# One-core transformer block in split fp32: the lists' matmuls a step deeper, their key products on ScalarE, gate tiles of a pair loaded ahead, the last two query tiles interleaved, the static split and the overflow set-up moved

## The chip, the core and the metric

The kernel runs on one core of a Trainium2 chip. Engines are named as in the profile: PE (TensorE), DVE (VectorE), ACT (ScalarE), POOL (GpSimd), SP (SyncE, which here only issues DMAs). The metric is the device time of one launch in microseconds (us); the median of the runs counts.

## The reference, cut to what matters

A block of attention and a PEER layer (product-key mixture of single-row experts), then a second block (gated convolution and linear recurrence). All of it is fp32 on 256 tokens of width 2048. The change touches the PEER layer:

```python
q = (xt @ w_query).reshape(T, 8, 2, 128)
scores = jnp.einsum('thpc,hpnc->thpn', q, sub_keys)      # 128 keys per half
vals, idx = lax.top_k(scores, 16)                        # per token, head, half
cand = vals[..., 0, :, None] + vals[..., 1, None, :]     # 256 candidates
top_vals, top_c = lax.top_k(cand, 16)
experts = i1 * 128 + i2                                  # 128 (expert, gate) pairs per token
gates = softmax(top_vals)
hdn = gelu(einsum('ted,td->te', expert_down[experts], x))
y = einsum('te,ted->td', gates * hdn, expert_up[experts])
```

## The kernel before

A product in fp32 is made of three: every operand is split into a high part (a cast to fp32r) and a low part (the rest), and PE multiplies high by high, high by low and low by high. `Stream` (line 63) feeds the weights: a unit is 128 x 2048 fp32 (1 MB), loaded by SP into one of three buffers `raw`, and then split in two halves into `whl` (five buffers): the high part is an ACT cast (line 74), the low part a DVE subtraction (line 75). So a half is ready at most five halves ahead of its use. `fm` (line 88, matmuls on lines 100 to 102) multiplies one unit with all 256 tokens in 48 matmuls; `tm` (line 106) does it with tokens as rows.

The PEER layer (`phase_peer`) takes no gather for its first product: it computes the hidden value of all 16384 experts for all 256 tokens. Its parts, in the order of PE:

1. 16 query tiles (loop on line 898), each `fm`, then the scores of the tile before. The top-k work (DVE and POOL) is cut in steps in a queue `k.bg`; `pump_by` (line 187) takes as many steps after each unit as a credit in us, and the `us` that each step names, allow. In the last tile (g 15) the activations `k.act` are replaced, quarter by quarter, by their scaled form (`split`, lines 213 and 214), since the next units need that form.
2. 128 down units in groups of four (loop on line 1013; a group `j` is 512 experts). `hidden` (line 978) writes the gelu of a unit into `ghs` (three buffers, one per group). In the background run, first, the steps `place_steps` (matmuls, line 710) that scatter each token's gates into a full table `g_d` in HBM. As long as it isn't complete, finished groups go to `gh_d` in HBM and into the queue `late` (23 groups). Once it is (`state["placed"]`), `catch_up` (line 996) brings the late ones back, one or two at a time: POOL loads the gates of a pair of groups (`gt<-g_d`, line 875, 1 MB, for every second group) and the group (`ght<-gh_d`, line 890), multiplies (`times`, line 880) and stores to `hm_d` (line 883). The last nine groups, called direct here (23 to 29, then 31 and 30), are multiplied from `ghs`; the gates of their pair are loaded by `hidden` right before the first of the pair is multiplied, into one buffer `gtd`. All of that stands in POOL's one queue in program order. Group JS = 31 isn't stored: its product is split into `hst` (lines 213 and 214), the left operand of the first four up units.
3. From down unit 103 on, the background builds lists of the experts in use: 32 steps `lists_steps` (line 848). Step q issues `lists_hot(q+2)` (two DVE comparisons, tiles `oe` and `oa`, lines 826 and 828), `lists_keys(q+1)` (tile `ob`: one half an ACT product, line 836, the other a DVE product, line 837) and `lists_fill(q)` (four PE matmuls, line 845). What is left after unit 123 is drained.
4. A branch over code that isn't run with these inputs (`overflow`, lines 1058 to 1090): each engine loads a register (line 1063) and jumps (line 1064). DVE prepares two tiles for it first, `ld` (line 1060) and `xe` (line 1062).
5. 104 up units (matmuls on line 1117): four static ones (they use `hst`), then 100 whose rows POOL gathers by the lists (line 1047).

Of the kernel before, what the change touches and what calls it, by code (L numbers as in the profile page):

```python
# [26 lines left out]
NE = 128  # L27
# [4 lines left out]
JS = 31  # L32
# [15 lines left out]
class Stream:  # L48
# [29 lines left out]
    def next(self):  # L78

        self.i += 1  # L80
        while self.done < min(2 * self.i + HL - 2, 2 * len(self.units)):
            self._half()
        return self.w.pop(self.i - 1)

    def used(self):
# [477 lines left out]
def phase_peer(k, A):  # L563
# [5 lines left out]
    with ExitStack() as ctx:  # L569
# [250 lines left out]

        def lists_hot(q):
            cs = slice(4 * q, 4 * q + 4)
            a = pw.tile([128, 4, 128], F32R, name="oa", tag="oa", bufs=3)
            e = pw.tile([128, 4, KT], F32, name="oe", tag="oe")
            rp = L["rp"]
            nc.vector.tensor_tensor(e, iota[:, None, :KT].to_broadcast([128, 4, KT]),
                                    rp[:, 0, cs, None].to_broadcast([128, 4, KT]), op=OP.is_equal)
            nc.vector.tensor_tensor(a, iota[:, None, :].to_broadcast([128, 4, 128]),
                                    rp[:, 1, cs, None].to_broadcast([128, 4, 128]), op=OP.is_equal)
            hot[q] = [a, e]  # L830

        def lists_keys(q):
            cs = slice(4 * q, 4 * q + 4)
            b = pw.tile([128, 4, 2, KT], F32R, name="ob", tag="ob")
            e = hot[q][1]
            nc.scalar.mul(b[:, :, 0, :], e, pi)
            nc.vector.tensor_mul(b[:, :, 1, :], e, iota[:, cs, None].to_broadcast([128, 4, KT]))
            hot[q][1] = b

        def lists_fill(q):  # L840
            if q == 0:
                L["ps"] = bank(k, "bg")
            a, b = hot.pop(q)
            for j in range(4):
                nc.tensor.matmul(L["ps"][:, :2 * KT], a[:, j, :], b[:, j].rearrange("p e r -> p (e r)"),
                                 start=q + j == 0, stop=q == 31 and j == 3)

        def lists_steps(q):
            if q + 2 < 32:
                lists_hot(q + 2)  # L850
            if q + 1 < 32:
                lists_keys(q + 1)
            lists_fill(q)

        def indices(v, n, nm):

# [38 lines left out]
            nc.vector.tensor_sub(lo[:, t], x[:, t], hi[:, t].bitcast(F32))  # L895

        scaled = []
        for g in range(16):
            w = st.next()
            acc = bank(k, "acc")[:, :256]  # L900
            if g == 15:
                for q in range(4):
                    fm(k, acc, w, k.act, part=(4 * q, 4 * q + 4))
                    qs = slice(4 * q, 4 * q + 4)
                    split(k, k.act[0][:, qs, :], k.act[1][:, qs, :], scaled.pop(0))
            elif g == 0:
# [12 lines left out]
            if g == 4:  # L919
                row_bc(k, Rb, r)  # L920
            qT = pw.tile([128, 256], F32, name="qT", tag="qT")
            nc.scalar.copy(qT, acc)
            if g < 2:
                pump(k)
            else:
                pump_by(k, 3.2)
            if 6 <= g <= 12 and g % 2 == 0:

                q = g // 2 - 3
                x = pw.tile([128, 4, 256], F32, name="xr", tag="ob" if q == 3 else "ghs", bufs=2 if q == 3 else 3)  # L930
                a, b = [o[:, 4 * q:4 * q + 4, :].bitcast(F32) for o in k.act]
                nc.gpsimd.tensor_add(x, a, b)
                nc.gpsimd.tensor_mul(x, x, Rb[:, None, :].to_broadcast([128, 4, 256]))
                scaled.append(x)
            k.bg.appendleft(step(0.0, lambda g=g, qT=qT: scores(g, qT)))
            if g % 2:
                k.bg.extend(topk_steps(g // 2))
        state = {}

        def prepare():  # L940

            def lag():
# [28 lines left out]
            yield step(1.5, lambda: lists_hot(0))  # L971
            yield step(2.2, lambda: (lists_hot(1), lists_keys(0)))
            for q in range(32):
                yield step(2.2, lambda q=q: lists_steps(q))
            yield lag()
            yield step(1.5, lists_end)
        k.bg.extend(prepare())
# [3 lines left out]
        def hidden(j, a, gh, acc):  # L981
# [7 lines left out]
            if state.get("g") != j // 2:  # L989
                state["g"], state["gt"] = j // 2, load_g(j // 2, "gtd")  # L990
            times(gh, state["gt"], j)
            if j == JS:
                hst = state["hst"] = pp.tile([128, 2, 4, 256], F32R, name="hst", tag="gst%d" % (JS // 2 % 2))
                split(k, hst[:, 0], hst[:, 1], gh)
            else:
                store(j, gh)

# [57 lines left out]
        k.gather = gather  # L1055


        def overflow():
            d = L["d"]
            nc.vector.tensor_scalar(d, d, -128.0 * KT, None, op0=OP.add)  # L1060
            ex = pw.tile([128, 128], F32, name="xe", tag="xe", bufs=1)
            nc.vector.tensor_scalar(ex, iota, 128.0, pi, op0=OP.mult, op1=OP.add)
            turns = nc.values_load(L["nx"][0:1, 1:2], min_val=0, max_val=NE)
            with k.tc.If(turns > 0), k.tc.For_i(0, turns, 1) as _:
                ps = bank(k, "bg")
                for c in range(NE):
                    a = pw.tile([128, 128], F32, name="xa", tag="xa")
                    nc.vector.tensor_scalar(a, iota, d[:, c:c + 1], None, op0=OP.is_equal)
                    nc.tensor.matmul(ps[:, :1], a, ex[:, c:c + 1], start=c == 0, stop=c == NE - 1)
                v = pp.tile([128, 1], F32, name="xv")  # L1070
                nc.vector.tensor_copy(v, ps[:, :1])
                idx = indices(v, 1, "x")
                x = pw.tile([128, 2048], F32, name="xu", tag="xu", bufs=1)
                get(x, up, idx[:, 0, :], NE * 128)
                y = pw.tile([128, 256], F32, name="xh", tag="hr", bufs=4)
                get(y, hm_d, idx[:, 1, :], JS * 512 + 1)
                h = pw.tile([128, 2, 256], F32R, name="xs", tag="hh", bufs=3)
                split(k, h[:, 0], h[:, 1], y)
                for c in range(4):
                    cs = slice(c * 512, (c + 1) * 512)  # L1080
                    w = pw.tile([128, 2, 512], F32R, name="xw", tag="xw", bufs=1)
                    split(k, w[:, 0], w[:, 1], x[:, cs])
                    for t in range(2):
                        ts = slice(t * 128, (t + 1) * 128)
                        o = bank(k, "bg")
                        for i, (p, q) in enumerate(((0, 0), (0, 1), (1, 0))):
                            nc.tensor.matmul(o, h[:, p, ts], w[:, q], start=i == 0, stop=i == 2)
                        nc.vector.tensor_add(k.h[:, t, cs], k.h[:, t, cs], o)
                nc.vector.tensor_scalar(d, d, -128.0, None, op0=OP.add)
        overflow()  # L1090

        accs = [[bank(k, "bg" if c < 2 else "acc") for t in range(2)] for c in range(4)]
# [619 lines left out]
```

## Time and profile before

| | us |
|---|---|
| median of three runs | 2737.36 |
| lowest run | 2737.03 |
| the profiled execution: its time | 2741.86 |
| its span, from the first to the last instruction | 2740.1 |
| PE busy in that span | 2634.3 (96%) |
| DVE busy | 1829.5 (67%) |
| ACT busy | 1411.4 (52%) |
| POOL busy | 738.6 (27%) |

Times in the rows are us from the start of the span. Where PE waits, two things cost: the wait itself and, after a longer one, matmuls at the lower granted clock. An engine's share over the whole span says little here, since the stages have different limits: the query tiles lie at about 464 to 579 us, the down units at 573 to 1408, the lists at 1186 to 1362, and the up units begin at 1421.5.

### The profile page before, as it was taken

What the parts mean: (1) busy time and instruction counts of PE and PEld (TensorE: products, weight loads), DVE (VectorE), ACT (ScalarE), POOL (GpSimd) and SP (SyncE); (2) the same over time, 40 slices, a digit from 0 to 9 for tenths busy, and PEclk for the clock granted to TensorE, in tenths of its full rate; (3) what the DMA queues carried; (4) which work ended last, traced back from release to release, by engine and by line L of the source; (5) the groups of instructions that cost most, each with busy time, mean ns of one, the idle gap of its engine ahead of it and who ended that gap; (6) DMA issues with size and microseconds to landing.
All of it is one profiled execution on the core that took longest, in us unless ns stands there. A gap on an engine that the chain in (4) does not pass through costs nothing. (4 is left out here: it accounts for less than half of the span.)

```text
span 2740.1 us, 44958 instructions
## 1 busy us (share of the span) xinstructions
PE 2634.3 (96%) x18008; PEld 2409.1 (88%) x18008; DVE 1829.5 (67%) x2685; ACT 1411.4 (52%) x2302; POOL 738.6 (27%) x779
## 2 busy tenths in 40 slices
PE   8999999989999999989759999999999999999997
PEld 8977778989999999989748888887999999999886
DVE  5554455899777877688826666666568775555555
ACT  6344455544566666434325555556665544444453
POOL 0001011532000000255625555645145540000000
PEclk9999999999999999999879999999999999999999
DMA  7433435456688888989847888885544445555553
GB/s 290 169 123 139 155 118 188 155 171 214 208 279 274 279 279 289 312 308 340 303 146 271 297 292 293 293 300 173 191 167 156 153 154 204 185 185 188 185 192 127
DMA packets 95268, 599.11 MB, mean 219 GB/s; under 512 B 11536, under 2 KB 11664, under 8 KB 31952
## 3 DMA queue, kind: packets, MB, share of 16 engines
q1 hardware_dynamic: 53696, 381.05, 39.6%
q0 software_dynamic: 36608, 200.23, 21.6%
q10 hardware_dynamic: 4752, 14.92, 1.5%
q8 instruction: 143, 2.34, 0.3%
q14 instruction: 69, 0.57, 0.1%
HBM read 532.19 MB, written 47.19 MB: 211 GB/s over the span
## 5 line engine op out<-in xcount | busy, mean ns | idle before, releaser
L75 DVE TENSOR_TENSOR whl<-raw,whl 128x1024 fp32r<-128x1024 f32 (+2 forms) x917 | 1188.5, 1306 | 633.7 <-ACT whl L74 623.0
L74 ACT CAST whl<-raw 128x1024 fp32r<-128x1024 f32 (+2 forms) x917 | 954.3, 1048 | 734.2 <-PE acc L102 381.4
L100 PE MATMUL acc<-act,whl 128*128 128x256 f32 x3840 | 1083.4, 282 | 17.8 <-ACT whl L74 17.6
L101 PE MATMUL acc<-act,whl 128*128 128x256 f32 x3840 | 1081.8, 282 | 9.1 <-DVE act L214 8.7
L102 PE MATMUL acc<-act,whl 128*128 128x256 f32 x3840 | 1081.6, 282 | 0.8 <-DVE whl L75 0.8
L100 PEld LDWEIGHTS acc<-act,whl 128*128 128x128 f32 x3840 | 729.4, 190 | 20.2 <-ACT whl L74 17.8
L101 PEld LDWEIGHTS acc<-act,whl 128*128 128x128 f32 x3840 | 730.1, 190 | 10.0 <-DVE act L214 8.9
L102 PEld LDWEIGHTS acc<-act,whl 128*128 128x128 f32 x3840 | 733.3, 191 | 1.3 <-DVE whl L75 1.3
L1117 PE MATMUL acc<-whl,hh 128*128 128x512 f32 x864 | 218.2, 396 | 0.0
L1117 PE MATMUL bg<-whl,hh 128*128 128x512 f32 x864 | 217.9, 396 | 0.0
L118 PE MATMUL acc<-whl,act 128*128 128x512 f32 (+1 forms) x512 | 198.2, 387 | 6.9 <-ACT whl L74 6.9
L119 PE MATMUL acc<-whl,act 128*128 128x512 f32 (+1 forms) x512 | 196.1, 383 | 4.0 <-DVE whl L75 3.9
L1117 PEld LDWEIGHTS bg<-whl,hh 128*128 128x128 f32 x864 | 162.5, 188 | 39.3
L1117 PEld LDWEIGHTS acc<-whl,hh 128*128 128x128 f32 x864 | 162.4, 188 | 39.2
L120 PE MATMUL acc<-whl,act 128*128 128x512 f32 (+1 forms) x512 | 195.8, 382 | 0.8 <-DVE act L217 0.8
L1047 POOL DMA_INDIRECT raw<-in_up,idx_l x100 | 134.1, 1341 | 150.5 <-DVE hh L895 77.6
L118 PEld LDWEIGHTS acc<-whl,act 128*128 128x128 f32 x512 | 97.5, 190 | 28.7 <-ACT whl L74 7.4
L119 PEld LDWEIGHTS acc<-whl,act 128*128 128x128 f32 x512 | 97.5, 190 | 24.4 <-DVE whl L75 5.8
L738 POOL DMA_DIRECT2D g_d<-gst x16 | 8.9, 556 | 395.7 <-DVE gst L722 395.7
L120 PEld LDWEIGHTS acc<-whl,act 128*128 128x128 f32 x512 | 97.4, 190 | 20.2 <-DVE act L217 1.0
L1047 POOL DMA_INDIRECT hr<-hm_d,idx_l x100 | 104.4, 1044 | 31.0 <-issue 30.7
L700 ACT ACTIVATE ob<-oe,sl_g 128x128 fp32r<-128x128 f32 x256 | 81.5, 391 | 8.1 <-ACT ghs L982 6.5
(407 smaller groups left out, 3071.5 us busy)
## 6 DMA issues: line engine op xcount, KB each, us to landing
raw<-in_down SPq DMA_DIRECT2D x128, 1024.0 KB, 6.3
raw<-in_w_cv SPq DMA_DIRECT2D x32, 1024.0 KB, 4.8
raw<-in_w_gg SPq DMA_DIRECT2D x32, 1024.0 KB, 4.8
raw<-in_w_dil SPq DMA_DIRECT2D x24, 1024.0 KB, 4.9
gt<-g_d POOLq DMA_DIRECT2D x17, 1024.0 KB, 10.7
raw<-in_w_out SPq DMA_DIRECT2D x16, 1024.0 KB, 4.8
raw<-in_w_pq SPq DMA_DIRECT2D x16, 1024.0 KB, 4.9
g_d<-gst POOLq DMA_DIRECT2D x16, 1024.0 KB, 7.8
```

The source lines that it names most:

```text
L74: nc.scalar.copy(hi[:, s], r[:, s])
L75: nc.vector.tensor_sub(lo[:, s], r[:, s], hi[:, s].bitcast(F32))
L100: k.nc.tensor.matmul(acc, hi[:, f], x, start=j == 0, stop=False)
L101: k.nc.tensor.matmul(acc, hi[:, f], y, start=False, stop=False)
L102: k.nc.tensor.matmul(acc, lo[:, f], x, start=False, stop=j == nk - 1)
L118: k.nc.tensor.matmul(accs[t], ah[:, kk, ts], hi[:, m], start=st, stop=False)
L119: k.nc.tensor.matmul(accs[t], ah[:, kk, ts], lo[:, m], start=False, stop=False)
L120: k.nc.tensor.matmul(accs[t], al[:, kk, ts], hi[:, m], start=False, stop=sp)
L700: nc.scalar.mul(b[:, j, 0, :], e[:, j, :], slot["g"][:, 0, 4 * q + j:4 * q + j + 1].bitcast(F32))
L738: nc.gpsimd.dma_start(g_d[g], x.rearrange("p i t -> p (i t)"))
L1047: nc.gpsimd.indirect_dma_start(out=out, out_offset=None, in_=table, in_offset=bass.IndirectOffsetOnAxis(ap=idx, axis=0), bounds_check=n - ...
L1117: nc.tensor.matmul(accs[2 * s + c][t], x[:, ts], y[:, c * 512:(c + 1) * 512], start=i == 0 and x is hh and y is hi, stop=last_ and i == N - 1)
```

## The change

Six edits. (a) `lists_steps(q)` issues the matmuls of step q-1, so each product is made two steps ahead of its use; a fourth buffer for `oa` and a third for `ob` come from tiles that are free by then. (b) The DVE product of the keys goes to ACT: six ACT operations per step (two of 128 x 2 x 100, four of 128 x 100) in place of one of 128 x 400; a step's cost for the credit falls from 2.2 to 1.7. (c) After a direct group, if the next group belongs to another pair, the gates of that pair are loaded at once. (d) Query tiles 14 and 15 run interleaved by quarters, and each quarter of `k.act` is split as soon as both have used it; behind tiles 14 and 15 one background step is taken instead of 3.2 us of them. (e) The split into `hst` is issued three units later. (f) `ld` and `xe` are made inside the branch.

```diff
+    def peek(self):
+        self.i += 1
         return self.w.pop(self.i - 1)
...
         def lists_hot(q):
-            a = pw.tile([128, 4, 128], F32R, name="oa", tag="oa", bufs=3)
+            a = (pp.tile([128, 4, 128], F32R, name="oa", tag="sl_g") if q % 4 == 3 else
+                 pw.tile([128, 4, 128], F32R, name="oa", tag="oa", bufs=3))
...
         def lists_keys(q):
-            b = pw.tile([128, 4, 2, KT], F32R, name="ob", tag="ob")
+            if q % 3 == 2:
+                b = [pw.tile([128, 2, 2, KT], F32R, name="ob", tag="oh") for _ in range(2)]
+            else:
+                b = pw.tile([128, 4, 2, KT], F32R, name="ob", tag="ob")
+                b = [b[:, 0:2], b[:, 2:4]]
             e = hot[q][1]
-            nc.scalar.mul(b[:, :, 0, :], e, pi)
-            nc.vector.tensor_mul(b[:, :, 1, :], e, iota[:, cs, None].to_broadcast([128, 4, KT]))
+            for i in range(2):
+                nc.scalar.mul(b[i][:, :, 0, :], e[:, 2 * i:2 * i + 2], pi)
+            for j in range(4):
+                nc.scalar.mul(b[j // 2][:, j % 2, 1, :], e[:, j, :], float(4 * q + j))
...
         def lists_steps(q):
...
-            lists_fill(q)
+            if q >= 1:
+                lists_fill(q - 1)
...
         for g in range(16):
...
+            if g == 14:
+                pair = [(acc, w), (bank(k, "acc")[:, :256], st.peek())]
                 for q in range(4):
-                    fm(k, acc, w, k.act, part=(4 * q, 4 * q + 4))
+                    for o, x in pair:
+                        fm(k, o, x, k.act, part=(4 * q, 4 * q + 4))
+                    if q == 1:
+                        st.used()
+                        st.used()
                     qs = slice(4 * q, 4 * q + 4)
                     split(k, k.act[0][:, qs, :], k.act[1][:, qs, :], scaled.pop(0))
...
+            elif g < 14:
+                pump_by(k, 3.2)
             else:
-                pump_by(k, 3.2)
+                pump(k)
...
             times(gh, state["gt"], j)
+            n = ORDER.index(j) + 1
+            if n < 32 and ORDER[n] // 2 != j // 2:
+                state["g"], state["gt"] = ORDER[n] // 2, load_g(ORDER[n] // 2, "gtd")
             if j == JS:
                 hst = state["hst"] = pp.tile([128, 2, 4, 256], F32R, name="hst", tag="gst%d" % (JS // 2 % 2))
-                split(k, hst[:, 0], hst[:, 1], gh)
+                after(k, 3, lambda: split(k, hst[:, 0], hst[:, 1], gh))
...
         def overflow():
             d = L["d"]
-            nc.vector.tensor_scalar(d, d, -128.0 * KT, None, op0=OP.add)
-            ex = pw.tile([128, 128], F32, name="xe", tag="xe", bufs=1)
-            nc.vector.tensor_scalar(ex, iota, 128.0, pi, op0=OP.mult, op1=OP.add)
             turns = nc.values_load(L["nx"][0:1, 1:2], min_val=0, max_val=NE)
-            with k.tc.If(turns > 0), k.tc.For_i(0, turns, 1) as _:
+            with k.tc.If(turns > 0):
+                nc.vector.tensor_scalar(d, d, -128.0 * KT, None, op0=OP.add)
+                ex = pw.tile([128, 128], F32, name="xe", tag="xe", bufs=1)
+                nc.vector.tensor_scalar(ex, iota, 128.0, pi, op0=OP.mult, op1=OP.add)
+                with k.tc.For_i(0, turns, 1) as _:
+                    overflow_tile(d, ex)
```

The body of the loop is the new function `overflow_tile`, otherwise unchanged. Lines after the change are 5 to 33 higher (line 880 is 893, line 213 is 218).

Three places in the order of the instructions. First DVE, from the first weight subtractions beside query tile 14 on (`act` are the activations, `xr` their scaled form, `vals`, `tk`, `idx` and `oh` belong to the top-k steps). Before:

```order
L75 TENSOR_TENSOR whl<-raw,whl 128x1024 x2
L597 MAX vals<-sc 128x8
L598 MATCH_REPLACE tk<-vals,sc 128x128
L599 MAX_INDEX idx<-vals,sc 128x8
L632 TENSOR_TENSOR oh<-abf,cst 128x512
L602 MAX vals<-tk 128x8
L603 MAX_INDEX idx<-vals,tk 128x8
L75 TENSOR_TENSOR whl<-raw,whl 128x1024
L214 TENSOR_TENSOR act_82<-xr,act_81 128x1024 x3
L75 TENSOR_TENSOR whl<-raw,whl 128x1024
L214 TENSOR_TENSOR act_82<-xr,act_81 128x1024
```

And at the same place on DVE in the changed kernel:

```order
L75 TENSOR_TENSOR whl<-raw,whl 128x1024
L219 TENSOR_TENSOR act_82<-xr,act_81 128x1024
L75 TENSOR_TENSOR whl<-raw,whl 128x1024 x2
L219 TENSOR_TENSOR act_82<-xr,act_81 128x1024 x2
L75 TENSOR_TENSOR whl<-raw,whl 128x1024
L219 TENSOR_TENSOR act_82<-xr,act_81 128x1024
L75 TENSOR_TENSOR whl<-raw,whl 128x1024 x4
```

The four splits moved ahead of the top-k step, between the weight subtractions; everything ahead of this piece stands as before.

Second POOL, at the end of the down units, from the last late groups (`ght`) to the last direct ones (`ghs`: 28 and 29, then 31 and 30). Before:

```order
L880 TENSOR_TENSOR ght<-ght,gt 128x1024
L883 DMA hm_d<-ght 128x4x256
L875 DMA gt<-g_d 128x16x128
L880 TENSOR_TENSOR ghs<-ghs,gt 128x1024
L883 DMA hm_d<-ghs 128x4x256
L880 TENSOR_TENSOR ghs<-ghs,gt 128x1024
L883 DMA hm_d<-ghs 128x4x256
L875 DMA gt<-g_d 128x16x128
L880 TENSOR_TENSOR ghs<-ghs,gt 128x1024 x2
L883 DMA hm_d<-ghs 128x4x256
L1063 TENSOR_LOAD nx
```

The same end of POOL's queue in the changed kernel (group 28 stands further up, three late groups earlier):

```order
L893 TENSOR_TENSOR ght<-ght,gt 128x1024
L896 DMA hm_d<-ght 128x4x256
L893 TENSOR_TENSOR ght<-ght,gt 128x1024
L896 DMA hm_d<-ght 128x4x256
L893 TENSOR_TENSOR ghs<-ghs,gt 128x1024
L888 DMA gt<-g_d 128x16x128
L896 DMA hm_d<-ghs 128x4x256
L893 TENSOR_TENSOR ghs<-ghs,gt 128x1024 x2
L896 DMA hm_d<-ghs 128x4x256
L1115 TENSOR_LOAD nx
```

The gate load of the last pair moved past one instruction, the store of group 29; the product of group 31 still follows it directly.

Third ACT, from the gelu of down unit 123 to the branch (`hst` is the static split, `nx` the branch's count). Before:

```order
L982 ACTIVATE ghs<-acc 128x256
L213 CAST hst<-ghs 128x1024
L74 CAST whl<-raw 128x1024 x2
L982 ACTIVATE ghs<-acc 128x256
L74 CAST whl<-raw 128x1024 x2
L982 ACTIVATE ghs<-acc 128x256
L74 CAST whl<-raw 128x1024 x2
L982 ACTIVATE ghs<-acc 128x256 x2
L1063 TENSOR_LOAD nx
```

And in the changed kernel, from the same gelu on:

```order
L1007 ACTIVATE ghs<-acc 128x256
L74 CAST whl<-raw 128x1024 x2
L1007 ACTIVATE ghs<-acc 128x256
L74 CAST whl<-raw 128x1024 x2
L1007 ACTIVATE ghs<-acc 128x256
L218 CAST hst<-ghs 128x1024
L74 CAST whl<-raw 128x1024 x2
L1007 ACTIVATE ghs<-acc 128x256 x2
L1115 TENSOR_LOAD nx
```

The static cast moved behind four weight casts and two gelus; two weight casts still stand behind it. Elsewhere on PE, the last of the `place_steps` matmuls stand behind 93 down units (before: 91), and the first list matmuls behind 106 (before: 103).

## Rows read from the trace of the kernel before

**Rows 1.** PE's waits: us in total, times, longest.

```profile
PE bg L845 <- DVE ob L837: 26.2, 9, 6.7
PE acc L100 <- ACT whl L74: 17.6, 1, 17.6
PE bg L1117 <- DVEq L1064: 13.3, 1, 13.3
PE acc L101 <- DVE act L214: 8.7, 1, 8.7
PE bg L845 <- ACT ob L836: 5.3, 1, 5.3
```

**Rows 2.** Stretches: length, busy us (instructions) by engine, PE clock, DMA share, GB/s.

```profile
1130.00:1140.00 10.00, 10.00 (x88) 10.00 (x87) 2.40 (x2) 3.96 (x6) 2.28 (x3) 1.00 1.00 314
1250.00:1260.00 10.00, 8.44 (x73) 8.30 (x72) 9.90 (x12) 3.42 (x5) 5.72 (x3) 1.00 1.01 410
1130.00:1396.00 266.00, 219.25 (x1762) 217.39 (x1760) 195.15 (x193) 92.50 (x129) 139.69 (x101) 0.92 0.87 307
1186.00:1362.00 176.00, 144.51 (x1134) 143.00 (x1134) 151.78 (x138) 66.49 (x95) 103.99 (x75) 0.92 0.92 327
```

**Rows 3.** Groups of POOL's products, 1120 to 1400 us: busy, mean ns | idle before.

```profile
L880 POOL TENSOR_TENSOR ght<-ght,gt 128x1024 f32<-128x1024 f32 x23 | 63.6, 2764 | 51.9 <-DMA ght<-gh_d 51.7
L880 POOL TENSOR_TENSOR ghs<-ghs,gt 128x1024 f32<-128x1024 f32 x8 | 20.0, 2499 | 62.5 <-DMA gt<-g_d 31.5 <-issue 18.5 <-ACT ghs L982 12.5
```

**Rows 4.** Timeline of POOL: start, duration, engine, operation, [idle before].

```profile
1130.83 1.21 POOL L875 DMA_DIRECT2D gt<-g_d  x1 [7.03 <-DMA g_d<-gst]
...
1146.66 2.52 POOL L880 TENSOR_TENSOR ght<-ght,gt 128x1024 f32<-128x1024 f32 x1 [13.55 <-DMA ght<-gh_d]
...
1307.20 1.17 POOL L875 DMA_DIRECT2D gt<-g_d  x1
...
1317.76 2.63 POOL L880 TENSOR_TENSOR ght<-ght,gt 128x1024 f32<-128x1024 f32 x1 [4.79 <-DMA ght<-gh_d]
...
1321.48 1.16 POOL L875 DMA_DIRECT2D gt<-g_d  x1
...
1379.36 2.37 POOL L880 TENSOR_TENSOR ghs<-ghs,gt 128x1024 f32<-128x1024 f32 x1 [9.43 <-DMA gt<-g_d]
...
1386.47 1.17 POOL L875 DMA_DIRECT2D gt<-g_d  x1
1393.95 2.33 POOL L880 TENSOR_TENSOR ghs<-ghs,gt 128x1024 f32<-128x1024 f32 x1 [6.31 <-DMA gt<-g_d]
```

**Rows 5.** Tile gt: its DMAs from issue to landing.

```profile
DMA to landing us min/median/max: 7.3/10.7/19.5
```

**Rows 6.** Timeline of DVE: the last sum over the placed gates.

```profile
1138.83 2.29 DVE L744 TENSOR_REDUCE F<-fsum 128x128 f32<-128x2048 f32 x1 [6.28 <-DMA fsum<-gst]
```

**Rows 7.** Timeline of ACT, DVE and PE: from the static split to the up units.

```profile
1396.32 1.04 ACT L213 CAST hst<-ghs 128x1024 fp32r<-128x1024 f32 x1 [28.20 <-POOL ghs L880]
...
1398.54 2.36 DVE L75 TENSOR_TENSOR whl<-raw,whl 128x1024 fp32r<-128x1024 f32 x2
...
1415.12 0.52 DVE L1062 TENSOR_SCALAR xe<-cst 128x128 f32<-128x128 f32 x1 [7.77 <-DMA hm_d<-ghs]
...
1421.53 0.77 PE L1117 MATMUL bg<-whl,hst 128*128 128x512 f32 x1 [13.26 <-DVEq L1064]
```

**Rows 8.** Timeline of DVE and PE around the last query tile.

```profile
563.53 2.36 DVE L75 TENSOR_TENSOR whl<-raw,whl 128x1024 fp32r<-128x1024 f32 x2
...
569.69 3.48 DVE L214 TENSOR_TENSOR act<-xr,act 128x1024 fp32r<-128x1024 f32 x3
...
579.10 0.27 PE L590 MATMUL bg<-keys,qT 128*128 128x128 f32 x1
```

**Rows 9.** Groups of ACT's key products (the first from 1186 to 1362 us).

```profile
L836 ACT ACTIVATE ob<-oe,cst 128x400 fp32r<-128x400 f32 x31 | 19.2, 622 | 27.2 <-DVE oe L826 21.1 <-PE bg L845 6.1
...
L700 ACT ACTIVATE ob<-oe,sl_g 128x128 fp32r<-128x128 f32 x256 | 81.5, 391 | 8.1 <-ACT ghs L982 6.5
```

More of the change, by code (lines that the diff above doesn't have):

```diff
@@ L82, in next @@
             self._half()
+        return self.w.pop(self.i - 1)
+    def peek(self):
+        self.i += 1
         return self.w.pop(self.i - 1)
@@ L844, in lists_fill @@
             for j in range(4):
-                nc.tensor.matmul(L["ps"][:, :2 * KT], a[:, j, :], b[:, j].rearrange("p e r -> p (e r)"),
+                nc.tensor.matmul(L["ps"][:, :2 * KT], a[:, j, :], b[j // 2][:, j % 2].rearrange("p e r -> p (e r)"),
                                  start=q + j == 0, stop=q == 31 and j == 3)
@@ L897, in phase_peer @@
         scaled = []
+        pair = []
         for g in range(16):
-            w = st.next()
-            acc = bank(k, "acc")[:, :256]
-            if g == 15:
-                for q in range(4):
-                    fm(k, acc, w, k.act, part=(4 * q, 4 * q + 4))
+            if g < 15:
+                w = st.next()
+                acc = bank(k, "acc")[:, :256]
+            if g == 14:
+                pair = [(acc, w), (bank(k, "acc")[:, :256], st.peek())]
+                for q in range(4):
+                    for o, x in pair:
[3 more added lines that the diff above has]
+                        st.used()
                     qs = slice(4 * q, 4 * q + 4)
                     split(k, k.act[0][:, qs, :], k.act[1][:, qs, :], scaled.pop(0))
+            elif g == 15:
+                acc = pair[1][0]
             elif g == 0:
@@ L970, in prepare @@
             yield step(1.6, lists_split)
[L971 to L974, printed above, removed]
+            yield step(1.7, lambda: lists_hot(0))
+            yield step(1.7, lambda: (lists_hot(1), lists_keys(0)))
+            for q in range(33):
+                yield step(1.7, lambda q=q: lists_steps(q))
             yield lag()
@@ L1055, in phase_peer, with overflow_tile @@
         k.gather = gather
+        def overflow_tile(d, ex):
+            ps = bank(k, "bg")
+            for c in range(NE):
+                a = pw.tile([128, 128], F32, name="xa", tag="xa")
+                nc.vector.tensor_scalar(a, iota, d[:, c:c + 1], None, op0=OP.is_equal)
+                nc.tensor.matmul(ps[:, :1], a, ex[:, c:c + 1], start=c == 0, stop=c == NE - 1)
+            v = pp.tile([128, 1], F32, name="xv")
+            nc.vector.tensor_copy(v, ps[:, :1])
+            idx = indices(v, 1, "x")
+            x = pw.tile([128, 2048], F32, name="xu", tag="xu", bufs=1)
+            get(x, up, idx[:, 0, :], NE * 128)
+            y = pw.tile([128, 256], F32, name="xh", tag="hr", bufs=4)
+            get(y, hm_d, idx[:, 1, :], JS * 512 + 1)
+            h = pw.tile([128, 2, 256], F32R, name="xs", tag="hh", bufs=3)
+            split(k, h[:, 0], h[:, 1], y)
+            for c in range(4):
+                cs = slice(c * 512, (c + 1) * 512)
+                w = pw.tile([128, 2, 512], F32R, name="xw", tag="xw", bufs=1)
+                split(k, w[:, 0], w[:, 1], x[:, cs])
+                for t in range(2):
+                    ts = slice(t * 128, (t + 1) * 128)
+                    o = bank(k, "bg")
+                    for i, (p, q) in enumerate(((0, 0), (0, 1), (1, 0))):
+                        nc.tensor.matmul(o, h[:, p, ts], w[:, q], start=i == 0, stop=i == 2)
+                    nc.vector.tensor_add(k.h[:, t, cs], k.h[:, t, cs], o)
+            nc.vector.tensor_scalar(d, d, -128.0, None, op0=OP.add)
@@ L1058, in overflow @@
         def overflow():
             d = L["d"]
-            nc.vector.tensor_scalar(d, d, -128.0 * KT, None, op0=OP.add)
-            ex = pw.tile([128, 128], F32, name="xe", tag="xe", bufs=1)
-            nc.vector.tensor_scalar(ex, iota, 128.0, pi, op0=OP.mult, op1=OP.add)
             turns = nc.values_load(L["nx"][0:1, 1:2], min_val=0, max_val=NE)
-            with k.tc.If(turns > 0), k.tc.For_i(0, turns, 1) as _:
[L1065 to L1089, printed above, removed]
```

1 line of the change is left out of this document (removed).

## Prediction

> **What bounds the kernel now.** I read PE's waits first, since PE is busy for 96% of the span. Seventy us of it can be named [rows 1]: list matmuls wait for DVE's key product (26.2 us, nine times) and for ACT's (5.3), one weight unit waits 17.6 us for ACT's cast, the up units wait 13.3 us for DVE's branch, and the last query tile waits 8.7 us for a split. The second view is the table of stretches [rows 2]: over the lists PE's granted clock is 0.92, a mean between the two levels (2.4 and 1.2 GHz), where quiet stretches show 1.00. That is 8% of 176 us, 14.1 us of matmuls at the lower level after waits. So PE could win 70 + 14 us at most, if nothing else came late.
>
> The third view shows what else comes late. ACT's static split idles 28.20 us for POOL [rows 7], and behind it in ACT's order stand two weight casts: that is PE's 17.6. POOL multiplies the last late groups while PE is nearly through the down units [rows 4]: POOL is tens of us behind PE, in one queue, and its idle time is DMA waits: 51.9 us for late groups and 62.5 for gates of direct groups [rows 3]. One cycle of two late groups lasts from 1307.20 to 1321.48, 14.3 us, of which 4.79 are a visible wait and the rest two products, two stores and three issues [rows 4]. So POOL's chain sets when group 31's product is there, 1396.28 (1393.95 + 2.33), and from that the up units follow. Below, T is the end of this product in the changed kernel.
>
> **The change, part by part.** *Lists (a, b).* Each key product is made one step earlier, so the 26.2 and the 5.3 go; with them most of the 14.1 us of slow clock. DVE loses 32 products. ACT gains, per step, at least the removed form (0.62 us, the mean of one 128 x 400 product) and at most 2 x 0.622 + 4 x 0.391 = 2.8 us, by the nearest rows [rows 9]. The instructions issued back to back there cost 0.32 each (81.5/256), which gives about 2 us. That is 32 x 2 = 64 us more on ACT, which is busy 66.49 of the 176 us [rows 2]; weights are cast up to five halves ahead, so I cost it at nothing. Without that cover it would be a wait of 2 us a step. On PE these edits bring the end of the down units forward: it lies at 1408.27 (1421.53 - 13.26 [rows 7]), and less 26.2, 5.3, 14.1 and the 17.6 of the next part it becomes about 1345.
>
> *Static split moved (e).* It no longer stands ahead of four of the six weight casts, and the two behind it are for weights that the down units don't need. The 17.6 go as a wait for weights. But the up units need `hst`, thus T: the stall isn't gone if T is late, it moves from the last down unit to the first up unit.
>
> *Gates ahead (c).* What is T? The last placing matmuls stand two units later, 48 matmuls each: 5.45 us a unit at 88 in 10 us, 6.0 at 1762 in 219 with slow clock [rows 2]; with 5.6 that is 11.2 us. DVE's last sum ends at 1141.12 (1138.83 + 2.29 [rows 6]); plus 11.2, plus a gate landing of 10.7 [rows 5], plus a product of 2.4: the first direct product ends at 1165.4. In the old trace the work from the first gate load (1130.83) to the last pair's load (1368.76 = 1379.36 - 9.43 - 1.17) takes 237.9 us [rows 4]. From this go the direct waits before the last two, 62.5 - 9.43 - 6.31 = 46.7, since their gates are now loaded a pair ahead; the first wait, 15.83 (1146.66 - 1130.83), since the late groups are loaded beside the first direct one; and to it come three waits for late groups that the long direct waits had covered, 3 x 4.79 = 14.4. That leaves 189.8 and ends at 1355.2. The last pair gains nothing: its gates are asked for right behind 29's product and needed at once, so 2.4 + 10.7 + 2.35 follow, T = 1371.
>
> The other bound is the traffic. From 1130 to 1396 the core moved 307 GB/s, 81.7 MB [rows 2]; with the last store of `g_d` and `fsum` (1 MB each) it is 83.8 MB, and the share was 0.87. At full share and the same work, 307/0.87 = 353 GB/s, it takes 237 us, T = 1367; at the 327 GB/s of the list stretch, 256 us, T = 1386 [rows 2]. I take T = 1378, between the two and near the chain's sum, as prefetches ask for more at once and landings should not get shorter. The ends kept are 1355 and 1396.
>
> The Trainium skill ("DMA: Bandwidth & Descriptors", section Specifications) gives a limit of about 358 GB/s of HBM traffic for a core; by it the bytes above would need 234 us, an estimate that gives T = 1364. The 353 GB/s at full share agree, and one stretch with 410 GB/s [rows 2] stands above it, so the rule is no floor here.
>
> POOL's late products take 2764 ns on average and 2.33 us where nothing runs beside them [rows 3, 4]; if the absence of DVE's key products made them all short, 23 x 0.43 = 10 us at most would come off the chain, T = 1361. The Trainium skill ("SBUF — State Buffer", section Who interferes with whom) says that DVE and GpSimd share one port pair and that this is an exclusive lock; by it the 32 products that leave DVE speak for that shorter chain, but the weight subtractions, far more numerous, stay.
>
> *From T to the up units.* Before, product to the end of DVE's second weight subtraction is 1398.54 + 2.36 - 1396.28 = 4.6 us [rows 7]: the cast, two weight casts and the subtractions, the same instructions in both. *The branch (f)*: without `xe` DVE no longer waits 7.77 us for the store; what remains is 1421.53 - 1415.64 = 5.9 us from the end of `xe` (1415.12 + 0.52) to the first up matmul [rows 7]. So the up units start at T + 10.5 = 1388.5 where before it was 1421.53. The gain is **33 us**, and PE waits some 43 us, from 1345 to 1388.
>
> *Query tiles (d).* DVE's order from 563.53 on now alternates weight subtractions (2.36/2 = 1.18) and splits (3.48/3 = 1.16) [rows 8]: four of each, 9.4 us, then a last group of 12 matmuls (1.4 us by 88 in 10 us [rows 2]) end at 574.4, where before the scores of the last tile come at 579.10 [rows 8]. I take **4 us**. The ends are 0 (the top-k steps moved behind make another wait) and 8.7 plus as much slow clock again at a quarter, about 11.
>
> Sum: 2740.1 - 33 - 4 = 2703.1 of span. The profiled execution, 2741.86, is 4.5 above the median 2737.36, so against the median: 2737.36 - 37 = **2700**.
>
> **Rivals.**
> *A: POOL's chain keeps up and PE loses all its waits.* 26.2 + 5.3 + 17.6 + 8.7, of the 13.3 all but the branch's 5.9, and the 14.1 of clock: 79.3 us, 2658. For it: 115 us of POOL's DMA waits [rows 3] and one stretch of 410 GB/s. Against it: it needs T at 1340, thus 83.8 MB in 210 us, 399 GB/s throughout, while another stretch at full share moved only 314 [rows 2]. Chance 0.15.
> *B: the loads are the bound and nothing comes earlier.* The DMA engines show a share of 0.92 to 1.0 in the list stretch [rows 2]; a load asked for earlier then lands no earlier, the placing is two units late, and T stays about 1396. Gain: 1421.53 - (1396 + 10.5) = 15, plus 4: 2718. Against it: the 46.7 us in which POOL had nothing else to do. Chance 0.21.
> *C: slower.* Weights that PE takes without stalls and gates asked for earlier collide: a landing of gates goes above its median of 10.7; the old range is 7.3 to 19.5 [rows 5]. Some twelve pairs' loads stand in series in the chain, so each us more costs 12.5 us of T. From 13.3 on the 33 us are eaten, from 13.7 on the 4 of the tiles too; at 14.3, T = 1423, the up units start 12 us later than before and the time is 2745. Against it: the mean share of 0.87 leaves room. Chance 0.07.
>
> **How the numbers follow.** The forecast has 0.57 and its own range is 2686 (T = 1364) to 2712 (T = 1390). The range of 8 in 10 runs from 2658, A's centre, over B with some room, to 2728; outside are half of A, C and a little of B. A difference of 2% (below 2682.6 or above 2792) is about what a measurement of this kernel tells from no change. Faster by that: A, 0.15, and 0.05 for a forecast whose T falls under 1360 by the short products. Slower by that: C with landings near the old maximum, 0.02. Within: 0.78.
>
> **What would show it.** Right: list waits under 5 us in all; no wait for ACT's cast in the last down units; one wait of about 43 us ahead of the first up matmul; group 31's product on POOL at about 1378, directly behind a gate landing of some 10 us; the tile split's wait under 5 us. Wrong: a wait ahead of the up units below 10 us means A. A product of 31 near 1396 means B, and landings of `gt` with a median above 13 mean C. Waits of list matmuls or of weights for ACT mean that the key products weren't free there. New waits at the tiles behind query tile 15 mean that the delayed top-k work was needed.

## The result, and the profile after

| | before | changed |
|---|---|---|
| median | 2737.66 us | 2707.53 us |
| lowest run | 2737.03 | 2704.73 |
| profiled execution, span | 2741.86, 2740.1 | 2705.44, 2703.6 |

The ratio is 0.9886, with an interval of 0.987 to 0.9902: 1.1% faster. The medians are of four runs each; one of the four before took 6639.96 us, and the other three lie within 1 us of one another. The forecast was 2700, its own range 2686 to 2712. The span came out at 2703.6, where the sum had said 2703.1. That this is so close is partly luck: terms of the sum were wrong and nearly cancelled, as the section on the prediction shows.

PE's waits of the changed kernel (us in total, times, longest), to lay beside [rows 1]:

```profile
PE bg L1150 <- ACT whl L74: 26.4, 1, 26.4
PE bg L857 <- ACT ob L849: 14.6, 4, 10.4
...
PE acc L107 <- DVE whl L75: 3.6, 2, 3.4
PE bg L595 <- ACT qT L945: 1.0, 1, 1.0
```

The waits of 26.2, 17.6, 13.3 and 8.7 us are gone. In their place stands one of 26.4 ahead of the first up matmul: the stall moved from the last down unit to the up units, as foretold, though it is 26 us and not 43. List matmuls still wait 14.6 us, now for ACT. The 8.7 us at the last query tile became 3.4 for a weight half and 1.0 for `qT`.

POOL of the changed kernel: two groups (1120 to 1400 us; columns as in [rows 3]) and one of its waits (total, times, longest), then its timeline, as in [rows 4], and DVE's last sum:

```profile
L893 POOL TENSOR_TENSOR ght<-ght,gt 128x1024 f32<-128x1024 f32 x23 | 59.9, 2604 | 49.7 <-DMA ght<-gh_d 49.4
L893 POOL TENSOR_TENSOR ghs<-ghs,gt 128x1024 f32<-128x1024 f32 x9 | 22.9, 2545 | 27.1 <-DMA gt<-g_d 23.4 <-ACTq L1116 3.6
```

```profile
POOL ght L903 <- DMA hm_d<-ght: 13.2, 6, 3.5
```

```profile
1138.24 1.21 POOL L888 DMA_DIRECT2D gt<-g_d  x1 [6.84 <-DMA g_d<-gst]
...
1147.37 1.18 POOL L888 DMA_DIRECT2D gt<-g_d  x1 [6.84 <-DVE F L749]
1165.64 2.71 POOL L893 TENSOR_TENSOR ghs<-ghs,gt 128x1024 f32<-128x1024 f32 x1 [17.09 <-DMA gt<-g_d]
...
1367.74 1.19 POOL L888 DMA_DIRECT2D gt<-g_d  x1 [0.50 <-POOL ghs L893]
1368.93 0.76 POOL L896 DMA_DIRECT2D hm_d<-ghs  x1
1376.02 2.33 POOL L893 TENSOR_TENSOR ghs<-ghs,gt 128x1024 f32<-128x1024 f32 x1 [6.33 <-DMA gt<-g_d]
```

```profile
1144.78 2.29 DVE L749 TENSOR_REDUCE F<-fsum 128x128 f32<-128x2048 f32 x1 [4.56 <-DMA fsum<-gst]
```

POOL's idle time ahead of the direct products fell from 62.5 us to 27.1; 23.4 of it is waiting for gates, all of that for the first (17.09) and the last (6.33). One wait is new: POOL issues the load of a late group only when the store of an earlier product has landed, 13.2 us in six waits (before: 1.1 us, once). Group 31's product ends at T = 1376.02 + 2.33 = 1378.35; the forecast was 1378.

From T to the up units, ACT, DVE and PE (beside [rows 7]), and the wait of ACT that the list matmuls hang on:

```profile
1323.26 0.38 ACT L1007 ACTIVATE ghs<-acc 128x256 f32<-128x256 f32 x1 [17.23 <-DMA hm_d<-ghs]
...
1324.57 1.18 PE L857 MATMUL bg<-ob,oa 128*128 128x200 f32 x4 [10.41 <-ACT ob L849]
...
1378.39 1.04 ACT L218 CAST hst<-ghs 128x1024 fp32r<-128x1024 f32 x1 [20.75 <-POOL ghs L893]
...
1380.61 2.35 DVE L75 TENSOR_TENSOR whl<-raw,whl 128x1024 fp32r<-128x1024 f32 x2
...
1383.16 4.92 PE L1150 MATMUL bg<-whl,hst 128*128 128x512 f32 x12 [26.38 <-ACT whl L74]
```

The up units start 4.8 us behind T, 38.4 us earlier than before. The first two of these rows belong together. `ghs` has three buffers; ACT's gelu waits 17.23 us for one until POOL's store of an older group has landed. The key products stand behind that gelu in ACT's queue, and PE's list matmuls wait for them. So POOL's lag reaches PE in the lists too (earlier_spread, below, tests it).

The same stretches as in [rows 2]:

```profile
1130.00:1396.00 266.00, 225.04 (x1827) 221.52 (x1826) 181.46 (x171) 129.22 (x302) 146.34 (x109) 0.92 0.90 324
1186.00:1362.00 176.00, 156.20 (x1298) 155.19 (x1297) 136.10 (x117) 98.53 (x264) 110.02 (x82) 0.96 0.98 359
```

Over the lists the clock rose from 0.92 to 0.96 and the DMA share from 0.92 to 0.98. Last, the gelu of the first down unit, which shows what the query tiles gave: before, then changed.

```profile
584.94 0.39 ACT L982 ACTIVATE ghs<-acc 128x256 f32<-128x256 f32 x1
```

```profile
580.79 0.38 ACT L1007 ACTIVATE ghs<-acc 128x256 f32<-128x256 f32 x1
```

That is 4.15 us earlier, against 4 in the forecast.

### The profile page after: what moved, and what is told of

Its sections match the earlier page's. It is cut to its first block, busy times and chain, and to the rows that moved or that the text cites. A ratio compares the mean times of both kernels' runs of the same rounds, so it can differ in the third digit from the quotient of the medians.

```text
span 2703.6 us, 45079 instructions
## 1 busy us (share of the span) xinstructions
PE 2624.5 (97%) x18008; PEld 2398.8 (89%) x18008; DVE 1803.1 (67%) x2651; ACT 1437.9 (53%) x2462; POOL 737.0 (27%) x779
```

## Experiments

The theory: POOL's chain of late groups sets T and so the up units; the list steps bring little as long as that is so. The main rival: the list steps made the gain. A second question is what sets the pace of the chain, latencies in series or the DMA engines. The first four kernels were run beside one another (before: 2736.72), likewise the next four (2738.06) and the last four (2737.70).

**lists_alone.** The kernel before with the list edits only:

```diff
-            nc.vector.tensor_mul(b[:, :, 1, :], e, iota[...])
+            for j in range(4):
+                nc.scalar.mul(b[j // 2][:, j % 2, 1, :], e[:, j, :], float(4 * q + j))
...
-            lists_fill(q)
+            if q >= 1:
+                lists_fill(q - 1)
```

> The kernel before with only the list edits (a, b). If POOL's chain of late groups sets the up units, the list waits (26.2 and 5.3 us) go but come back as a longer wait behind the down units: group 31's product ends at 1396 within 6 us, the up units begin at 1421 within 6, time 2737 within 8. If the list steps are what the change gained, PE loses 31 us of waits and up to 14 of slow clock: 2692 to 2706.

Measured: 2741.51, ratio 1.0013 (1.0002 to 1.0024). No gain, rather a loss of 0.1%. PE's waits, then POOL, then DVE at the branch:

```profile
PE acc L100 <- ACT whl L74: 34.5, 2, 32.9
PE bg L851 <- ACT ob L843: 17.7, 4, 13.9
...
PE bg L1124 <- DVEq L1071: 8.6, 1, 8.6
```

```profile
1394.64 2.33 POOL L887 TENSOR_TENSOR ghs<-ghs,gt 128x1024 f32<-128x1024 f32 x1 [6.37 <-DMA gt<-g_d]
```

```profile
1415.72 0.51 DVE L1069 TENSOR_SCALAR xe<-cst 128x128 f32<-128x128 f32 x1 [7.68 <-DMA hm_d<-ghs]
1417.56 1.23 DVE L75 TENSOR_TENSOR whl<-raw,whl 128x1024 fp32r<-128x1024 f32 x1 [1.32 <-DVEq L1071]
```

The list waits shrank (31.5 to 18.6 us), and the wait ahead of the last down units grew from 17.6 to 32.9: T is 1396.97, as before (1396.28). The up units begin at 1417.5, 4 us earlier than in the profile of before, but only since the branch took 1.32 us behind `xe` here and not 5.94. As the main cause, the list steps fall; what they are worth with T out of the way is measured below.

**no_gates_ahead.** The changed kernel without (c):

```diff
-            n = ORDER.index(j) + 1
-            if n < 32 and ORDER[n] // 2 != j // 2:
-                state["g"], state["gt"] = ORDER[n] // 2, load_g(ORDER[n] // 2, "gtd")
```

> The changed kernel with the gates of a direct pair loaded only when needed (c undone). Chain theory: the direct gate waits return (46.7 us) less the waits for late groups they hide (14.4); with the placing two units later than before, group 31's product ends at 1400 to 1410 instead of 1378 and the time is 2725 to 2738. If the lists made the gain: 2705 to 2712, as the changed kernel.

Measured: 2730.89, ratio 0.9977 (0.9967 to 0.9987). The direct groups' waits are back:

```profile
L893 POOL TENSOR_TENSOR ghs<-ghs,gt 128x1024 f32<-128x1024 f32 x7 | 17.0, 2432 | 62.4 <-DMA gt<-g_d 46.0 <-ACT ghs L1007 16.4
```

```profile
1401.18 2.33 POOL L893 TENSOR_TENSOR ghs<-ghs,gt 128x1024 f32<-128x1024 f32 x1 [6.48 <-DMA gt<-g_d]
```

T = 1403.5, the up units begin 25.1 us later, and without the three lines of (c) 23.4 of the 30 us are lost. (What (c) brings alone, without the other edits, wasn't run.)

**lists_as_before.** The changed kernel with the list code of before (the first diff the other way round).

> The changed kernel with the list steps and the key product on DVE as before (a, b undone). Chain theory: the list waits grow from 14.6 to some 30 us but are paid out of the 26.4 us that PE waits ahead of the up units; that wait falls to 5 to 15 us, group 31's product stays at 1378 within 6, the time at 2705 to 2714. If the list steps matter by themselves, all of it shows: 2722 to 2738.

Measured: 2713.43, ratio 0.991 (0.9893 to 0.9926). Time and T are as the theory had them; the list waits are 38 us, more than the 30 expected, so that no wait for T is left ahead of the up units, where 5 to 15 us were expected.

```profile
PE bg L850 <- DVE ob L842: 38.2, 13, 8.3
...
PE bg L1142 <- PEq L1108: 2.5, 1, 2.5
```

The slack of 26.4 paid for most of it; what it didn't cover is the 6 us. (T is 1375.3 there, 1372.11 + 3.16, and the up units begin at 1392.7: PE itself is last.)

**place_faster.** A placing step costs 2.55 in the credit (2.9 in the changed kernel).

```diff
-                yield step(2.9, lambda q=q: place_steps(q))
+                yield step(2.55, lambda q=q: place_steps(q))
```

> The changed kernel with 2.55 in place of 2.9 as the cost of a placing step, which ends the placing 8 units earlier (85 for 93) and leaves 21 late groups for 23. Chain theory: POOL's chain starts some 45 us earlier and is no longer the last; the up units begin within 10 us of the end of the down units (about 1357), time 2678 to 2690. Rival: DVE, 80% busy during the placing, can't give the steps faster, PE waits there, and the time is 2700 or more; or the DMA engines, at a share of 0.98, let nothing end earlier than by the 3 MB saved, 9 us: 2697.

Measured: 2705.85, ratio 0.9886 (0.987 to 0.9903): no better than the changed kernel. A miss, with the rival's reason:

```profile
PE bg L715 <- DVE ob L703: 10.1, 6, 1.8
PE bg L857 <- ACT ob L849: 6.8, 1, 6.8
PE bg L715 <- ACT ob L705: 5.7, 2, 3.9
...
PE bg L1150 <- PEq L1116: 2.7, 1, 2.7
```

The wait ahead of the up units did go (26.4 to 2.7), but PE lost 15.8 us on the placing matmuls, which it hadn't lost at all, and the chain began 24 us earlier, not 45 (first gate load 1113.92 for 1138.24). PE ended the down units at 1383.2, 26 us later than in the changed kernel, so the last path had moved from POOL to PE.

**xe_outside.** `ld` and `xe` ahead of the branch again (f undone: the last part of the change's diff the other way round).

> The changed kernel with `ld` and `xe` made ahead of the branch again (f undone). In the changed kernel the store of the last group is issued at 1385.5 and PE starts the up units at 1383.2. If DVE's wait for that store and the 5.9 us behind it are real: the store lands at about 1389, the first up matmul is at 1395, 12 us later: 2714 to 2720. If `xe` only filled a gap that the branch leaves anyway: 2705 to 2710.

Measured: 2714.84, ratio 0.991 (0.9889 to 0.9931).

```profile
1392.01 0.52 DVE L1117 TENSOR_SCALAR xe<-cst 128x128 f32<-128x128 f32 x1 [3.69 <-DMA hm_d<-ghs]
1393.85 1.23 DVE L75 TENSOR_TENSOR whl<-raw,whl 128x1024 fp32r<-128x1024 f32 x1 [1.32 <-DVEq L1119]
```

DVE does wait for the store, and the up units begin at 1393.8, 12.4 us behind T (4.8 in the changed kernel); (f) is worth 7.3 us. Behind `xe` the branch takes 1.32 us, as in lists_alone. In the trace of before it is 5.94, the one case of the three:

```profile
1421.57 1.22 DVE L75 TENSOR_TENSOR whl<-raw,whl 128x1024 fp32r<-128x1024 f32 x1 [5.94 <-DVEq L1064]
```

**half_weights.** One execution only. The second half of the weights isn't loaded for 28 units.

```diff
-    u += [(A["down"][4 * j + a], 2048) for j in ORDER for a in range(4)]
+    u += [(A["down"][4 * j + a], 2048 if i < 25 else -2048) for i, j in enumerate(ORDER) for a in range(4)]
...
-                    nc.sync.dma_start(self.raw[:, s], ap[:, s])
+                    s = slice(0, 1024) if half else s
+                    nc.sync.dma_start(self.raw[:, s], ap[:, s])
```

> The changed kernel with only half of each weight unit loaded for the down units 100 to 127 (both halves are made from that half, so their hidden values aren't the reference's). 14.7 MB of loads go, none of them in POOL's queue. If the DMA engines set the pace of POOL's chain (share 0.98, 353 GB/s): 41 us less, group 31's product by 1350 and no wait of PE ahead of the up units. If the chain is a series of latencies: the product at 1368 to 1378, the wait still above 15 us.

Measured: 2687.31. POOL's instructions and their order are the same; only SP loads less. The last product, and the table of stretches from the first gate load to T, of this kernel, then of the changed one:

```profile
1349.37 3.43 POOL L895 TENSOR_TENSOR ghs<-ghs,gt 128x1024 f32<-128x1024 f32 x1 [7.80 <-ACT whl L76]
```

```profile
1138.00:1352.00 214.00, 198.39 (x1618) 196.83 (x1618) 190.35 (x159) 115.37 (x286) 135.49 (x101) 0.96 0.88 296
```

```profile
1138.00:1378.00 240.00, 204.20 (x1711) 203.19 (x1710) 167.57 (x161) 118.54 (x289) 135.69 (x101) 0.93 0.94 338
```

T = 1352.8, 25.5 us earlier and not 41, and it ends as a wait for ACT: there PE is last, and its wait ahead of the up units is 3.0. So the weight loads beside it did slow POOL's chain, by at least 25.5 us; fixed latencies alone would have left T near where it was.

**tiles_pump.** Behind query tiles 14 and 15 `pump_by(k, 3.2)` instead of `pump(k)`, so that the placing ends 2 units earlier.

> The changed kernel, but behind query tiles 14 and 15 the background again takes 3.2 us of steps and not one (that part of d undone): the placing ends 2 units earlier, behind 91. Chain theory: group 31's product 11 us earlier, at 1367, time 2692 to 2699. Rival: those steps on DVE stand ahead of the splits' successors, PE waits at the first down units, or the DMA engines give the time back: 2702 or more.

Measured: 2702.02, ratio 0.9865 (0.9844 to 0.9885), at the lower edge of the rival's range and 3 us above the chain theory's. The first gate load is 10.4 us earlier, T only 4:

```profile
1127.80 1.21 POOL L888 DMA_DIRECT2D gt<-g_d  x1 [7.13 <-DMA g_d<-gst]
...
1371.94 2.33 POOL L893 TENSOR_TENSOR ghs<-ghs,gt 128x1024 f32<-128x1024 f32 x1 [6.25 <-DMA gt<-g_d]
```

```profile
ACT ghs L1007 <- DMA hm_d<-ghs: 53.3, 4, 20.9
```

Some of the difference goes into ACT's gelu, which waits 53.3 us for POOL's stores (33.3 in the changed kernel), while POOL in turn waits 18.9 us for ACT. So the delay of the top-k steps in (d) costs the changed kernel some 5 us, if anything: the two intervals overlap.

**place_earlier.** tiles_pump, and 2.75 as the cost of a placing step.

> As tiles_pump, and a placing step costs 2.75 in place of 2.9: the placing ends behind 87 units (93 in the changed kernel), 33 us earlier. With 2.55 PE lost some 16 us of waits in the placing; here the steps go 5% faster, not 14%, so the waits should stay under 5 us. Chain theory: the product of 31 at 1350 or when PE has made the group, the up units right behind the down units: 2682 to 2692. Rival: the waits of the placing come back in full: 2700 or more.

Measured: 2693.36, ratio 0.9833 (0.9812 to 0.9854), 1.4 us above the range of the theory. The waits of the placing are 6.2 us, not under 5; 2.7 us are left ahead of the up units; what remains is POOL's lag, through ACT (PE's waits, then ACT's from 1180 us on):

```profile
PE bg L857 <- ACT ob L849: 16.5, 3, 10.3
...
PE bg L715 <- DVE ob L703: 3.4, 2, 1.7
PE bg L715 <- ACT ob L705: 2.8, 2, 1.7
```

```profile
ACT ghs L1007 <- DMA hm_d<-ghs: 20.5, 3, 13.6
```

**split_at_once.** (e) undone: `split(...)` in place of `after(k, 3, lambda: split(...))`.

> The changed kernel with the static split issued where it was (e undone), thus four weight casts behind it on ACT. Chain theory: group 31's product stays at 1378; PE waits for weights before it and has about one down unit left behind it, some 10 us at the lower clock, before the up units can begin: 2714 to 2719. If the split's place is worth nothing because PE waits for the same product either way: 2705 to 2710.

Measured: 2713.96, ratio 0.991 (0.9893 to 0.9926). T is 1379.6, and PE's long wait is back ahead of the last down unit:

```profile
1381.69 0.58 PE L105 MATMUL acc<-act,whl 128*128 128x256 f32 x1 [28.57 <-ACT whl L74]
```

So (e) is worth some 6 us, the unit that else lies behind T; 7 to 11 had been expected.

**tiles_plain.** tiles_pump with query tiles 14 and 15 one after the other, as before.

> As tiles_pump (2702.0), and query tiles 14 and 15 one after the other as before (all of d undone). If the interleaving is worth the 4 us that the first hidden units came earlier: 2704 to 2708, with PE's wait of 8.7 for the split of the last tile back. If those 4 us are only paid into the wait ahead of the up units (23 us in tiles_pump): 2700 to 2703.5.

Measured: 2703.14, ratio 0.9872 (0.9855 to 0.9888). The 8.7 us are back, and the up units begin at 1382.3 for 1379.1 in tiles_pump; yet the medians differ by 1.1 us, with overlapping intervals. The traces show where half of these 3.2 us go: from the last up matmul to the first product of `Q` and `K` in the second block it is 165.8 us here and 167.4 in tiles_pump. The work there is the same, but in tiles_pump PE's granted clock is 0.83 over one stretch of 10 us (1858.1 to 1868.1), where here it is 1.00 (1861.4 to 1871.4). All eleven traces with the tiles interleaved show this drop, none of the three without; why is open. What the interleaving is worth at the end is thus 1 to 2 us at most, and not clear of noise.

**earlier_old_lists.** place_earlier with the list code of before.

> As place_earlier (2693.4), with the list steps and the key product on DVE as before (a, b undone). There POOL's chain is no longer last. If that is why the list edits gained so little in the changed kernel, they must pay here: 26 to 38 us of list waits in place of 16.5, and slow clock behind them: 2706 to 2722. If the DMA engines or POOL set the end even here: 2690 to 2698.

Measured: 2708.73, ratio 0.9895 (0.9879 to 0.9912). Here the same list edits are worth 15 us; they were worth 6 in the changed kernel and nothing on their own (lists_alone).

```profile
PE bg L850 <- DVE ob L842: 25.5, 10, 4.0
```

**earlier_spread.** place_earlier, with late groups taken two in three units:

```diff
-            n = -(-len(late) // max(1, NE - 6 - i))
+            n = 1 if 3 * len(late) >= 2 * (NE - 8 - i) else 0
```

> As place_earlier, and the late groups are taken two in three units and not one in each, so that the last is done behind unit 120 or so. In place_earlier ACT's gelu still waits 20.5 us for the store of a direct group (POOL is behind) and the list matmuls 16.5 us for ACT. If POOL's lag is the cause, both go: ACT's wait under 5 us, list waits under 6, 2678 to 2688. Rival: late groups end too close to the up units and the last product is late again: 2692 or more.

Measured: 2677.60, ratio 0.9778 (0.9761 to 0.9794), below both kernels: 0.9778/0.9886 = 0.989 of the changed one. ACT's gelu no longer waits for a store, and with that the list matmuls' wait for ACT falls from 16.5 to 1.2 us. PE's waits, POOL's and PE's end, and the stretch of the chain:

```profile
PE bg L857 <- DVE oe L833: 5.0, 1, 5.0
...
PE bg L1150 <- PEq L1116: 2.7, 1, 2.7
PE bg L857 <- ACT ob L849: 1.2, 2, 1.0
```

```profile
1342.31 2.40 POOL L893 TENSOR_TENSOR ghs<-ghs,gt 128x1024 f32<-128x1024 f32 x1 [1.15 <-DMA gt<-g_d]
```

```profile
1356.65 4.54 PE L1150 MATMUL bg<-whl,hst 128*128 128x512 f32 x12 [2.65 <-PEq L1116]
```

```profile
1112.00:1345.00 233.00, 226.79 (x1920) 226.27 (x1920) 194.26 (x172) 131.17 (x305) 138.42 (x99) 0.99 0.98 358
```

T is 1344.7, ahead of PE's last down unit; PE's clock over the chain is 0.99 where it was 0.93. Nothing in this stretch holds PE for more than 5 us now.

What (c), (f), (e) and (a, b) lose when each is undone, 23.4, 7.3, 6.4 and 5.9 us, adds up to more than the 30 us that the change gained. Each was taken with the others in place, so part of what it is worth depends on them.

## Why the prediction was right, and where it was off

*What bounds.* "From that the up units follow" held. T was moved by the gates (no_gates_ahead, 25 us later), and the up units moved with it (25.1). It was moved by the loads beside it (half_weights, 25.5 earlier) and by its start and the spread of the late groups (earlier_spread, 33.6 earlier), and the up units came 18.0 and 26.5 us earlier, until PE's own end was last. Shortening the list waits without moving T gave nothing (lists_alone). Rival A needed T by 1340 and falls with 1378; B wanted the product near 1396. C's sign can't be read directly, as the trace of the changed kernel has no landing times of `gt`; the first gates took 18.3 us, the last pair's 8.3, and the median in no_gates_ahead is 11.6, under the 13 that C needed. The wait that should be above 10 us was 26.4; the two signs that failed are that wait's size (43) and the list waits (under 5 us foretold, 14.6 measured).

*T.* The value taken, 1378, was met to 0.4 us, in part by luck: it was picked between a chain sum and a traffic bound. The chain sum of 1371 was 7.4 short, and not for one reason. The last sum ended at 1147.07 instead of 1152.3, since, it seems, the tiles' 4 us bring the placing forward too. The first gates took 18.3 us (1147.37 to 1165.64), not the median of 10.7. From the first product to the last pair's load it was 199.4 us and not 192.2. The waits for late groups' loads aren't the reason: the sum had allowed some 52.5 for them (51.7, less 13.55 at the start, plus 14.4), and they came to 49.4. The 46.7 us of direct waits went, though [rows 3] put 12.5 of the direct waits down to ACT and not to gates. What the sum had at nothing is the 13.2 us in which those loads could not be issued because an earlier store hadn't landed. The last pair took 10.6 and not 13.05. The traffic fits: 338 GB/s x 240 us = 81.1 MB from 1138 on, for 83.8 MB foretold.

*From T to the up units.* This step failed: the 5.9 us put down to the branch. In the changed kernel PE starts 0.2 us behind the second subtraction (1380.61 + 2.35), and in the two traces of other kernels with `xe` outside the branch takes 1.32. So the up units came 4.8 us behind T and not 10.5, which is 5.7 less. The 5.94 were seen in one execution, which lay 4.5 us above its median. The extra 4.6 us would explain that, but it isn't shown, as the other runs of that kernel left no trace. If it is so, the 37 us should not have been taken off the median, which lacked these 4.5 already.

*Query tiles.* The 4 us came (4.15), but they were added to a T worked out without them; counted like for like, T was foretold at 1374 and came 4 us late. This cancels most of the 5.7; another 1.9 us are given back behind the start of the up units (38.4 there, 36.5 in the span), most of it at the drop of the clock in the second block that tiles_plain shows: 167.3 us there against 165.7 before. So the span missed by 0.5 us; of the 7.5 by which the median misses 2700, 4.5 are the offset above, 2.1 the distance of the changed kernel's median from its own profiled run, and the rest that 0.5 and rounding.

*Lists.* "The 26.2 and the 5.3 go" held for DVE's part; 14.6 us came anew, for ACT. The price of the key products was not the reason: they took 0.80 us for the two of 128 x 200 and 0.80 for the four of 128 x 100, some 1.5 us a step against 2 foretold. The step that failed here is the cover: weights were looked at, the gelu that waits for a buffer ahead of the key products in ACT's queue wasn't. In earlier_spread, where that gelu doesn't wait, the key products cost PE 1.2 us. Of the 14.1 us of slow clock about half stayed (0.96 over the lists, and 4% of 176 us is 7.0). Both put off the end of the down units, which PE reached at 1356.8 and not 1345. All this cost little here, as PE waited 26.4 us for T anyway.

*The rules weighed.* The late products became shorter, by 0.16 us each here (2604 for 2764 ns, 3.7 us in all) and by 0.36 in lists_alone (2409). The Trainium skill ("SBUF — State Buffer", section Who interferes with whom) lets one expect that where DVE operations with two inputs in SBUF leave. That the same products leave DVE in both kernels, and the gain is more than twice as large in one, this doesn't explain. In lists_alone POOL's waits for late groups' loads grew (56.9 for 51.7) and T stayed, so the shorter products, 8.2 us in all, were worth nothing there. The DMA engines moved 358 GB/s over 233 us at a share of 0.98 in earlier_spread. The Trainium skill ("DMA: Bandwidth & Descriptors", section Specifications) names about 358 as the limit of a core. Over the 233 us that agrees, but 150 us of the same run moved more, so here it is no ceiling; a single stretch of 10 us lay above it before [rows 2].

```profile
1190.00:1340.00 150.00, 143.79 (x1207) 143.27 (x1207) 130.60 (x106) 92.15 (x233) 93.64 (x68) 0.98 0.99 366
```

## What to carry to other kernels

A wait that a change removes is worth something only if the work that it releases isn't itself queued for something later; follow the last waits to their common source (here POOL's chain, fed by loads) before pricing the others. The same edit (the lists) was worth nothing, 6 and 15 us, depending on how far that source had been dealt with. Where a chain was fed by DMA engines that were nearly full, starting it earlier and spreading it paid here (2677.60), and shorter instructions didn't (lists_alone); when loads are asked for earlier, look which buffer they then wait for; and check a term that rests on one execution (a branch, a first load) against that execution's distance from the median.

## What the runs showed of the hardware

Loads of a queue that works for other engines (SP) slowed POOL's products: 14.7 MB fewer of them brought the product of group 31 on POOL 25.5 us forward with POOL's own instructions unchanged (half_weights). A jump over a branch took DVE 5.94 us in one execution and 1.32 in two others of nearly the same code; why wasn't found. The granted clock fell to 0.83 over 10 us in the second block in eleven traces and stayed at 1.00 in three, with the same instructions and the same short waits there (2.05 us the longest); what the three have in common is that query tiles 14 and 15 stand one after the other, some 1300 us earlier, and the reason is open. A background step that comes 14% faster on a DVE that is 80% busy cost PE 15.8 us of waits (place_faster); at 5% faster it cost 6.2 (place_earlier).
